# Longer buffer slots, and one operand of the FFN matmuls moved by 32 bytes

## The chip, the cores and the metric

The kernel runs on one core of a Trainium2 chip. The metric is the device time of one execution in microseconds (us), as the median of several runs. A core has a matrix engine (TensorE, PE in the profile, with its weight loads listed apart as PEld), a vector engine (VectorE, DVE), a scalar engine for pointwise functions (ScalarE, ACT), GpSimd (POOL), and a queue that issues most of the DMA transfers (SyncE, SP). All engines work from SBUF, a memory of 128 partitions; where this document gives a place in bytes, it is the place within a partition. Matmuls write to PSUM, eight banks of 512 fp32 columns.

## The reference

One sequence of 512 tokens with 1024 features goes through two layers. Each layer is a token mixer followed by a dense SwiGLU FFN, and each of these four parts has a modulation of its own:

```python
shift, scale, gate = ada_modulation(c, ada_w[i], ada_b[i])
h = rms_norm(x, pre_g[i]) * (1.0 + scale) + shift
y = part(h)                 # attention, FFN, gMLP, FFN
x = x + gate * rms_norm(y, post_g[i])

def swiglu(h, w_gate, w_up, w_down):
    return (jax.nn.silu(h @ w_gate) * (h @ w_up)) @ w_down
```

The mixer of layer 0 is a stick-breaking attention of 16 heads, that of layer 1 a gMLP whose chunks of 128 tokens are mixed by a 128x128 matrix per channel group. The hidden width of the FFN is 2816. Everything is float32.

## The kernel before

**Precision.** Each float32 operand of a large matmul is split into two fp32r parts, a high part h and a low part l (`split`, L112: ScalarE copies, VectorE subtracts). A product is three matmuls, high by high, high by low and low by high (`mm3`, L104). In `mm(o, l, r)` (L92) l is the stationary operand, 128 columns of which are loaded into the array as weights before the matmul, and r the moving operand that streams through. The profile writes a matmul as result<-moving,stationary.

**Memory.** Tiles come from pools laid out one behind the other in each partition. Weights, after their split, lie in `wpool` (tiles wh and wl of 4096 bytes). Behind it the pool `s4` has 28 slots, handed out in turn by `slot` (L53): nearly all that lives longer than a moment is in one, such as h, the attention's operands, the FFN's activations, x, the modulation rows. A slot is 4096 bytes long. All slots and weight tiles start at multiples of 64 bytes.

**h in the FFN.** `boundary` (L419) finishes one part and prepares the next: it norms and modulates 128 tokens, transposes them on TensorE, and splits the result into slots hTh and hTl (L448), each with 4 blocks of 128 features by 256 tokens. `hB` (L413) returns one block, 256 columns or 1024 bytes per partition. Where the next part is an FFN, `boundary` also gets a dictionary S. `sums` (L459) fills it with the operands Sh and Sl (L466): four sums and differences of the quarters of h (two halves of the features by two halves of the tokens).

**The FFN.** The first three of 22 slices of the hidden width are computed directly (`Ffn.unit`, L1002, result gu): 2 x 8 products per 256 tokens. The other 19 go by a scheme with seven products of half size in place of eight (`Ffn.seven`, L1026): gate and up projections of a slice form a 2x2 block matrix, h the other, and the seven products use A11, A12, A22 (blocks of hT) and S1 to S4. Their weights are wh and wl, some of them sums built by `blocks` (L182), and two smaller tiles named b in the profile (b21). Each product is 4 blocks x 3 = 12 matmuls of 256 columns, so a slice is 84 matmuls, in three PSUM banks r1, r2, r3 (together r). In both forms the weights are stationary and h or S is moving:

```python
def product(o, a, b, start, stop):
    for k in range(4):
        h, l = S[a](k)
        wh, wl = W[b](k)
        mm3(o, wh, wl, h, l, start and k == 0, stop and k == 3)
```

Beside this, ScalarE and VectorE split the weights of the next slices, and the SP queue loads them. Where the FFN's down projection (`out_proj`, L491, result y; in the last layer X, Y, Z, W) and the gMLP's v run, it is the other way round: the activations are stationary and the weights are moving, mostly with 512 columns. The gMLP's h (also from `boundary`, with S left out) is moving in u (`u_unit`, L1239) and stationary in v.

The order on TensorE is that of the program; an engine's instructions run in order and wait for semaphores. DMA transfers of weights are issued a few tiles ahead (`wget`, L231), and rows of the modulation matrices (rawada) come in the background (`Bg.run`, L346), partly into slots.

Of the kernel before, what the change touches and what calls it, by code (L numbers as in the profile page):

```python
# [9 lines left out]
F32R = mybir.dt.float32r  # L10
# [3 lines left out]
P = 128  # L14
# [11 lines left out]
PAIRS = (tuple(range(NF)), (2, 4, 0, 6, 7, 1, 9, 10, 3, 5, 8))  # L26
SEVEN = ((2, 4, 6, 7, 9), (2, 4, 6, 7, 9, 10))
NLAST = 3


@with_exitstack
def trunk(ctx: ExitStack, tc: tile.TileContext, A: dict, out: bass.AP):
# [8 lines left out]
    s4 = ctx.enter_context(tc.tile_pool(name="s4", bufs=28))  # L41
# [7 lines left out]
    def nm(s):  # L49
        uid[0] += 1  # L50
        return f"{s}_{uid[0]}"

    def slot(dt, name, a=2, b=512):  # L53
        return s4.tile([P, a, b], dt, tag="s4", name=nm(name))

    def bank(name, tag="b"):
        return psum.tile([P, 512], F32, tag=tag, bufs=6 if tag == "b" else 2, name=nm(name))
# [42 lines left out]
    def transpose(o, i):  # L100
        last_tp[0] = nc.tensor.transpose(o, i, ident)  # L101
        pe_op(last_tp[0])
# [9 lines left out]
    def split(hi, lo, src, hi_dve=False):  # L112
        if hi_dve:
            dve.tensor_copy(hi, src)
        else:
            act.activation(hi, src, AF.Copy)  # L116
        dve.tensor_tensor(lo, src, hi.bitcast(F32), ALU.subtract)
# [177 lines left out]
    for tt in range(NT):  # L295
        xt = slot(F32, "x0", 1, 1024)
        load(xt[:, 0, :], A["x"][tt * P : (tt + 1) * P, :])
        x0.append(xt[:, 0, :])
        if tt == 0:
            identt = consts.tile([P, P], F32, name="identt")  # L300
            load(identt[:], A["consts"][:, 0, :])
            cols = consts.tile([P, 4, KD], F32, name="cols")
            load(cols[:], A["cols"])
        elif tt == 3:
            a0.extend(ada0_raw(0, q) for q in range(2))
# [23 lines left out]
    class Bg:  # L329
# [16 lines left out]
        def run(self):  # L346
            for name, at, s, part in self.parts:
                acc = slot(F32, name, 1, D)[:, 0, :]
                ada[name, at] = acc
                nc.gpsimd.memset(acc, 0.0)  # L350
                load(acc[0:1, :], A["adab"][s, part])
                raws = []
                for k in range(KD + self.lag):
                    if k < KD:
                        if self.slots:
                            raw = slot(F32, "rawada", 1, D)[:, 0, :]
                        else:
                            raw = fwork["raw"].tile([P, D], F32, tag="raw2", name=nm("rawada"))[:]
                        load(raw, A["ada"][s, part, k])
                        raws.append(raw)  # L360
                    if k >= self.lag:
                        ada_stt(acc, raws[k - self.lag], k - self.lag)
                    yield
# [29 lines left out]
    def rms(part, first=None):  # L393

        bias = epsb
        if first is not None:
            bias = small.tile([P, 1], F32, tag="ss", name=nm("ss"))
            dve.tensor_scalar(bias[:], first, 1.0 / D, EPS, ALU.mult, ALU.add)
        sd = small.tile([P, 1], F32, tag="sd", name=nm("sd"))
        last_sqrt[0] = act.activation(sd[:], part, AF.Sqrt, bias=bias[:], scale=1.0 / D)  # L400
        r = small.tile([P, 1], F32, tag="r", name=nm("r"))
        return sd, r

    def new_hT():
        return [
            (slot(F32R, "hTh"), slot(F32R, "hTl")) for _ in range(KD // 2)
        ]
# [11 lines left out]
    def boundary(s, tt, y, xin, hT, S, tag):  # L419

        halves = [slice(0, 512), slice(512, D)]
        sq = [small.tile([P, 1], F32, tag=f"sq{hf}", name=nm("sq")) for hf in range(2)]
        t = npool.tile([P, D], F32, tag="n", name=nm("t"))
        for hf, c in enumerate(halves):
            act.activation(junk[:, c], y[hf][:], AF.Square, accum_out=sq[hf][:])
            if hf == 1:
                sd, r2 = rms(sq[1][:], sq[0][:])
            dve.tensor_tensor(t[:, c], y[hf][:], ada["G", s][:, c], ALU.mult)
        dve.reciprocal(r2[:], sd[:])
        x = xin(tt)  # L430
        dve.scalar_tensor_tensor(x[:], t[:], r2[:, 0:1], x[:], ALU.mult, ALU.add)
        xd[tt] = dram.tile([P, D], F32, tag=f"x{tt}", bufs=2, name=nm("xd"))
        nc.gpsimd.dma_start(out=xd[tt][:], in_=x)
        sx = small.tile([P, 1], F32, tag="sx", name=nm("sx"))
        act.activation(junk[:], x[:], AF.Square, accum_out=sx[:])
        sd, r1 = rms(sx[:])
        dve.tensor_tensor(t[:], x[:], ada["A", s], ALU.mult)
        dve.reciprocal(r1[:], sd[:])
        dve.scalar_tensor_tensor(t[:], t[:], r1[:, 0:1], ada["B", s], ALU.mult, ALU.add)
        late = []  # L440
        for q in range(2):
            ps = bank("tp", tag)
            for k in range(4):
                kk = q * 4 + k
                transpose(ps[:, k * P : (k + 1) * P], t[:, kk * P : (kk + 1) * P])
            a = ps[:].rearrange("p (a b) -> p a b", a=4)
            if tt % 2 == 0:
                hT[tt // 2, q] = (slot(F32R, "hTh", 4, 256), slot(F32R, "hTl", 4, 256))  # L448
            c = slice(tt % 2 * P, (tt % 2 + 1) * P)
            th, tl = hT[tt // 2, q]  # L450
            split(th[:, :, c], tl[:, :, c], a)
            if S is not None and tt < 2:
                if tt == 0:
                    S["c", q] = slot(F32, "c", 4, 256)
                act.activation(S["c", q][:, :, tt * P : (tt + 1) * P], a, AF.Copy)
            late.append(a)
        return lambda: sums(S, tt, late)

    def sums(S, tt, a):  # L459

        if S is None or tt < 2:
            return
        c = slice((tt - 2) * P, (tt - 1) * P)
        if tt == 2:
            for n in "3214":
                S[n] = (slot(F32R, "Sh", 4, 256), slot(F32R, "Sl", 4, 256))  # L466
        f, g = [npool.tile([P, 2, 4, P], F32, tag="n", name=nm("fs")) for _ in range(2)]
        c0, c1 = [S["c", q][:, :, c] for q in range(2)]

        def part(n, f):  # L470
            split(S[n][0][:, :, c], S[n][1][:, :, c], f)

        dve.tensor_tensor(f[:, 0], c0, a[0], ALU.subtract)
        dve.scalar_tensor_tensor(f[:, 1], f[:, 0], -1.0, a[1], ALU.mult, ALU.subtract)
        dve.tensor_tensor(g[:, 0], f[:, 1], c0, ALU.add)
        part("1", g[:, 0])
        part("2", f[:, 1])
        dve.tensor_tensor(g[:, 1], f[:, 1], c1, ALU.add)
        part("4", g[:, 1])
        part("3", f[:, 0])  # L480
# [10 lines left out]
    def out_proj(s, nk, get_act, wkey, J, bg, hT, nxt=(), pre=None, S=None, steps=0, bg2=None):  # L491
# [61 lines left out]
        for n, tt in enumerate((2, 3)):  # L553
            if nxt:
                evacs.append(nxt[n]())
            late.append(boundary(s, tt, y[tt], xin, hT, S, "p" if tt == 3 else "b"))
# [9 lines left out]
    def sqrt_table():  # L566
        with tc.issue_after(last_act[0].ins):
            nc.scalar.preload_act_table_set("sqrt_and_others")
# [42 lines left out]
    hT = new_hT()  # L611
# [129 lines left out]
    with tc.tile_pool(name="att", bufs=1) as att, tc.tile_pool(name="att2", bufs=2) as att2:  # L741
# [60 lines left out]
        for js in (B31, B2, B0):  # L802
            at, n = {}, 0
# [4 lines left out]
            t = att.tile([P, -(-n // 16) * 16], F32, name=nm("ones"))[:, : n - 1]  # L808
# [182 lines left out]
    class Ffn:  # L991
# [97 lines left out]
        def last(self, bg0):  # L1089
# [70 lines left out]
            def common(banks):  # L1160

                us = []
                for s in range(2):
                    u = fpool.tile([P, 4, 256], F32, tag="f13", name=nm("u"))
                    z = [banks["Z", s][:, i * 256 : (i + 1) * 256] for i in range(2)]
                    w = [banks["W", s][:, i * 256 : (i + 1) * 256] for i in range(2)]
                    act.activation(u[:, 0, :], z[0], AF.Copy)
                    dve.tensor_tensor(u[:, 3, :], z[1], u[:, 0, :], ALU.add)
                    dve.tensor_tensor(u[:, 1, :], w[0], u[:, 3, :], ALU.add)
                    dve.tensor_tensor(u[:, 2, :], w[1], u[:, 3, :], ALU.add)  # L1170
                    dve.tensor_tensor(u[:, 3, :], w[0], u[:, 2, :], ALU.add)
                    us.append(u)
                return us
# [18 lines left out]
            for q in range(2):  # L1192
# [4 lines left out]
                for n, p in enumerate(PAIRS[q]):  # L1197
# [4 lines left out]
                    if p in SEVEN[q]:  # L1202
                        seven(now, W, banks, fresh)
                        if p == [i for i in PAIRS[q] if i in SEVEN[q]][-1]:
                            us = common(banks)
                    elif q == 1 and n >= NF - NLAST:
                        tail.append((p, now, W))
                    else:
                        for s in range(2):
                            eight(p, now, W, banks, s, (0, 1), ("X", s) in fresh)  # L1210
                            fresh -= {("X", s), ("Y", s)}
                    if q == 1 and n == NF - NLAST - 2:
                        sqrt_table()
# [278 lines left out]
```

## Time and profile before

| what | us |
|---|---|
| median of 3 runs | 1157.95 (1156.58 to 1157.99) |
| profiled execution | 1156.4 |
| its span, first to last instruction | 1154.6 |
| TensorE busy | 1133.0 |
| VectorE busy | 942.3 |
| ScalarE busy | 588.1 |

The granted clock of TensorE is 0.996 in the mean. The profile's groups of instructions give a line, an engine, an operation, result<-operands and the count, then busy time and the mean length of one in ns. A matmul is a pipeline: the profile's length of one is longer than the distance to the next, so the distance between starts is what counts. The chain of work that ended last lists pieces with their start, their length, and what they are; a piece of matmuls divided by its count gives the distance. Rows of a tile give the shortest, median and longest instruction in ns.

### The profile page before, as it was taken

How to read it: one execution, taken by the hardware profiler on the slowest of the kernel's cores; microseconds unless marked ns; L12 is line 12 of the kernel's file. 1: busy time of each engine (PE TensorE's matmuls, PEld its weight loads, DVE VectorE, ACT ScalarE, POOL GpSimd, SP SyncE). 2: the span in 40 equal slices, each digit the busy share in tenths (PEclk: the TensorE clock that was granted, in tenths of full speed). 3: DMA queues.
4: the chain of work that ended last, by engine and by line, in shares of the span. 5: the costliest groups of instructions: out<-in, count | busy, mean ns of one | idle time of the engine just before them, and what ended most of it. 6: DMA issues, size and time to landing. Idle time of an engine off the chain costs nothing.

```text
span 1154.6 us, 18784 instructions
## 1 busy us (share of the span) xinstructions
PE 1133.0 (98%) x7532; PEld 1022.3 (89%) x7532; DVE 942.3 (82%) x1214; ACT 588.1 (51%) x977; POOL 23.9 (2%) x43
## 2 busy tenths in 40 slices
PE   6999999999999999999999999999999999999997
PEld 4778888788999999998877898988999999999996
DVE  4988999866998889879686955668979898789996
ACT  6444454645655555554142633526555555565752
POOL 0010000000000000000000100001000000000000
PEclk9999999999999999999999999999999999999999
DMA  8855433114425343338887465324333433223242
GB/s 313 330 183 170 140 111 128 73 56 146 146 92 165 129 148 127 119 118 279 276 283 239 149 231 168 111 70 155 106 125 129 164 129 125 77 91 94 90 163 94
DMA packets 50812, 174.43 MB, mean 151 GB/s; under 512 B 5786, under 2 KB 9114, under 8 KB 50724
## 3 DMA queue, kind: packets, MB, share of 16 engines
q1 hardware_dynamic: 48996, 166.94, 42.7%
q0 software_dynamic: 1728, 6.29, 1.4%
q8 instruction: 59, 0.97, 0.3%
q14 instruction: 29, 0.24, 0.1%
HBM read 164.82 MB, written 8.39 MB: 150 GB/s over the span
## 4 chain that ended last, share of the span: by engine, by line
PE 84%; DMA 6%; DVE 6%; ACT 2%; issue 1%; SPq 0%; DVEq 0%; ACTq 0%
PE r L93 33%; PE y L93 9%; PE v L93 8%; PE pqk L93 7%; PE gu L93 5%; DMA rawada<-in_ada 4%; PE X L93 4%; PE Y L93 3%; PE u L93 3%; PE av L93 3%; PE z L93 2%; PE W L93 1%; PE Z L93 1%; PE tw L101 1%; PE tp L101 1%
## 5 line engine op out<-in xcount | busy, mean ns | idle before, releaser
L93 PE MATMUL r<-Sh,wh 128*128 128x256 f32 x608 | 172.1, 283 | 0.0
L93 PE MATMUL r<-Sl,wh 128*128 128x256 f32 x608 | 172.1, 283 | 0.0
L93 PE MATMUL r<-Sh,wl 128*128 128x256 f32 x608 | 172.1, 283 | 0.0
L93 PE MATMUL y<-wh,as 128*128 128x512 f32 x480 | 150.8, 391 | 0.8 <-DVE G L69 0.8
L159 ACT ACTIVATE wh<-raw 128x1024 fp32r<-128x1024 f32 x87 | 91.6, 1058 | 116.3 <-PE y L93 58.6
L69 DVE TENSOR_TENSOR wl<-f,wh 128x1024 fp32r<-128x1024 f32 x87 | 106.2, 1220 | 39.8 <-ACT wh L116 39.8
L116 ACT ACTIVATE wh<-f 128x1024 fp32r<-128x1024 f32 x87 | 92.2, 1060 | 89.9 <-PE r L93 65.6
L160 DVE TENSOR_TENSOR wl<-raw,wh 128x1024 fp32r<-128x1024 f32 x87 | 105.8, 1219 | 38.5 <-ACT wh L159 34.5
L93 PEld LDWEIGHTS r<-Sh,wh 128*128 128x128 f32 x608 | 116.7, 192 | 0.0
L93 PEld LDWEIGHTS r<-Sl,wh 128*128 128x128 f32 x608 | 116.7, 192 | 0.0
L93 PEld LDWEIGHTS r<-Sh,wl 128*128 128x128 f32 x608 | 116.7, 192 | 0.0
L93 PEld LDWEIGHTS y<-wh,as 128*128 128x128 f32 x480 | 90.1, 188 | 19.7 <-DVE G L69 1.3
L93 PE MATMUL y<-wl,as 128*128 128x512 f32 x240 | 93.7, 390 | 0.0
L93 PE MATMUL r<-hTh,wh 128*128 128x256 f32 x304 | 87.8, 292 | 0.0
L93 PE MATMUL r<-hTl,wh 128*128 128x256 f32 x304 | 85.4, 282 | 0.0
L93 PE MATMUL r<-hTh,wl 128*128 128x256 f32 x304 | 81.0, 283 | 0.0
L93 PE MATMUL r<-hTh,b 128*128 128x256 f32 x304 | 61.0, 283 | 0.0
L93 PEld LDWEIGHTS r<-hTh,wh 128*128 128x128 f32 x304 | 57.9, 191 | 2.4 <-DVE gu L69 0.7
L93 PEld LDWEIGHTS r<-hTl,wh 128*128 128x128 f32 x304 | 58.1, 191 | 0.1
L116 ACT ACTIVATE wh<-rawx 128x1024 fp32r<-128x1024 f32 x38 | 40.3, 1060 | 33.9 <-PE r L93 31.8
L93 PEld LDWEIGHTS r<-hTh,wl 128*128 128x128 f32 x304 | 55.9, 191 | 0.0
L93 PE MATMUL gu<-hTh,wh 128*128 128x256 f32 x192 | 54.6, 285 | 0.0
(266 smaller groups left out, 3026.7 us busy)
## 6 DMA issues: line engine op xcount, KB each, us to landing
rawada<-in_ada SPq DMA_DIRECT2D x80, 512.0 KB, 4.6
rawy<-in_wy SPq DMA_DIRECT2D x38, 512.0 KB, 3.5
rawx<-in_wx SPq DMA_DIRECT2D x38, 512.0 KB, 4.3
raw<-in_wdown SPq DMA_DIRECT2D x22, 512.0 KB, 4.5
raw<-in_wdn SPq DMA_DIRECT2D x22, 512.0 KB, 3.5
raw<-in_wqk SPq DMA_DIRECT2D x16, 512.0 KB, 4.4
ada<-in_ada0p SPq DMA_DIRECT2D x12, 512.0 KB, 8.1
raw<-in_wgu SPq DMA_DIRECT2D x12, 512.0 KB, 3.5
```

The lines of the kernel that those rows point to most:

```text
L69: b = getattr(nc.vector, op)(*args, **kw)
L93: b = nc.tensor.matmul(o, l, r, start=start, stop=stop, skip_group_check=True)
L101: last_tp[0] = nc.tensor.transpose(o, i, ident)
L116: act.activation(hi, src, AF.Copy)
L159: act.activation(h[:], raw[:], AF.Copy)
L160: nc.vector.tensor_tensor(l[:], raw[:], h[:].bitcast(F32), ALU.subtract)
```

## The change

Slots of `s4` become 1040 fp32 elements (4160 bytes) long, that is 64 bytes longer. `slot` returns a view of the first 1024 elements, or of 1024 elements from `at` on. For the two FFNs, the slots of h (hTh, hTl) and of its sums (Sh, Sl from `sums`) are asked for with `at = 8` elements, 32 bytes. The h of the gMLP, and the operands named Sh and Sl that the last FFN's down projection builds for itself, stay at the start of their slots.

```diff
+ODD = 8
...
-    def slot(dt, name, a=2, b=512):
-        return s4.tile([P, a, b], dt, tag="s4", name=nm(name))
+    def slot(dt, name, a=2, b=512, at=0):
+
+        t = s4.tile([P, 1040], dt, tag="s4", name=nm(name))
+        return t[:, at : at + a * b].rearrange("p (a b) -> p a b", a=a)
...
             if tt % 2 == 0:
-                hT[tt // 2, q] = (slot(F32R, "hTh", 4, 256), slot(F32R, "hTl", 4, 256))
+                at = 0 if S is None else ODD
+                hT[tt // 2, q] = (slot(F32R, "hTh", 4, 256, at), slot(F32R, "hTl", 4, 256, at))
...
         if tt == 2:
             for n in "3214":
-                S[n] = (slot(F32R, "Sh", 4, 256), slot(F32R, "Sl", 4, 256))
+                S[n] = (slot(F32R, "Sh", 4, 256, ODD), slot(F32R, "Sl", 4, 256, ODD))
```

The 28 slots together take 28 x 64 = 1792 bytes more per partition; the pools behind them start that much later.

## The prediction

> **What bounds the kernel now.** I read the page first, then the groups of matmuls by shape, the chain of work that ended last, four stretches of time, and last the single starts of matmuls.
>
> ```profile
> span 1154.6 us, 18784 instructions
> PE 1133.0 (98%) x7532; PEld 1022.3 (89%) x7532; DVE 942.3 (82%) x1214; ACT 588.1 (51%) x977; POOL 23.9 (2%) x43
> ...
> PE r L93 33%; PE y L93 9%; PE v L93 8%; PE pqk L93 7%; PE gu L93 5%; DMA rawada<-in_ada 4%; PE X L93 4%; PE Y L93 3%; PE u L93 3%; PE av L93 3%; PE z L93 2%; PE W L93 1%; PE Z L93 1%; PE tw L101 1%; PE tp L101 1%
> ```
>
> TensorE has work in 98% of the span, and a third of the chain that ends last is the products called r, which are the middle of the two FFNs. The change touches the moving operand (named first after the arrow) of exactly these groups:
>
> ```profile
> L93 PE MATMUL r<-Sh,wh 128*128 128x256 f32 x608 | 172.1, 283 | 0.0
> L93 PE MATMUL r<-Sl,wh 128*128 128x256 f32 x608 | 172.1, 283 | 0.0
> L93 PE MATMUL r<-Sh,wl 128*128 128x256 f32 x608 | 172.1, 283 | 0.0
> ...
> L93 PE MATMUL r<-hTh,wh 128*128 128x256 f32 x304 | 87.8, 292 | 0.0
> L93 PE MATMUL r<-hTl,wh 128*128 128x256 f32 x304 | 85.4, 282 | 0.0
> L93 PE MATMUL r<-hTh,wl 128*128 128x256 f32 x304 | 81.0, 283 | 0.0
> L93 PE MATMUL r<-hTh,b 128*128 128x256 f32 x304 | 61.0, 283 | 0.0
> L93 PE MATMUL gu<-hTh,wh 128*128 128x256 f32 x192 | 54.6, 285 | 0.0
> L93 PE MATMUL gu<-hTh,wl 128*128 128x256 f32 x192 | 54.3, 283 | 0.0
> L93 PE MATMUL gu<-hTl,wh 128*128 128x256 f32 x192 | 54.3, 283 | 0.0
> ...
> L93 PE MATMUL r<-hTl,b 128*128 128x256 f32 x152 | 43.0, 283 | 0.0
> ```
>
> That is 3 x 608 + 4 x 304 + 152 = 3192 matmuls r and 3 x 192 = 576 matmuls gu. The 283 ns is a matmul with its pipeline. What it costs is the distance from one start to the next, which the chain gives as length over count:
>
> ```profile
> 306.58 22.31 PE gu L93 x186
> 328.89 181.34 PE r L93 x1500
> ...
> 743.85 6.65 PE sv L93 x60
> ...
> 762.84 25.04 PE y L93 x110
> ...
> 815.20 22.32 PE gu L93 x186
> 837.52 181.37 PE r L93 x1500
> ```
>
> A 256-column matmul costs 22.31 / 186 = 119.9 ns (gu) and 181.34 / 1500 = 120.9 ns (r). One of 512 columns costs 25.04 / 110 = 227.6 ns (y). So 256 columns more cost 107.7 ns, or 0.42 ns each, and 119.9 - 107.7 = about 12 ns per matmul do not depend on its length. The change can reach these 12 ns. One of 128 columns costs 6.65 / 60 = 110.8 ns (sv), far over 54 + 12: there another thing sets the pace, the load of 128 columns of weights that each matmul has, so 110.8 ns is the floor for the 256-column matmul too.
>
> ```profile
> 329.00:511.00 182.00, 182.00 (x1506) 181.18 (x1505) 153.02 (x206) 97.42 (x162) 0.00 (x0) 1.00 0.39 127
> 837.00:1019.00 182.00, 182.00 (x1507) 181.22 (x1506) 150.79 (x201) 96.97 (x162) 0.00 (x0) 1.00 0.37 122
> 815.00:837.00 22.00, 22.00 (x186) 22.00 (x185) 21.40 (x33) 11.28 (x18) 0.00 (x0) 1.00 0.22 74
> 292.00:329.00 37.00, 36.96 (x309) 36.72 (x308) 35.51 (x49) 22.55 (x39) 1.68 (x3) 1.00 0.43 146
> ```
>
> The columns are TensorE, weight loads, VectorE, ScalarE, GpSimd, granted clock, DMA. In the two r stretches (first two rows) TensorE is busy all the time at full clock, VectorE for 153.02 / 182 = 84%. Whatever a start costs there goes straight into the span. In the gu stretch at 815 us VectorE is busy 21.40 of 22 us, so a gain there is partly hidden behind it; a loss is not.
>
> The starts at the beginning of a block of r, where TensorE had waited:
>
> ```profile
> 338.71 0.39 PE L93 MATMUL r<-hTh,wh 128*128 128x256 f32 x1
> 338.94 0.28 PE L93 MATMUL r<-hTl,wh 128*128 128x256 f32 x1
> 339.05 0.29 PE L93 MATMUL r<-hTh,wl 128*128 128x256 f32 x1
> 339.18 0.28 PE L93 MATMUL r<-hTh,wh 128*128 128x256 f32 x1
> 339.29 0.28 PE L93 MATMUL r<-hTl,wh 128*128 128x256 f32 x1
> 339.41 0.28 PE L93 MATMUL r<-hTh,wl 128*128 128x256 f32 x1
> 339.53 0.28 PE L93 MATMUL r<-hTh,wh 128*128 128x256 f32 x1
> ```
>
> After the wait the distances are uneven (0.11 to 0.13 us), and then they lock at 0.12 us and stay there. Same instructions, same operands, different distance: some of the 12 ns depends on how the reads of the moving operand and of the next weights fall against each other.
>
> **The change part by part.** No instruction is added, removed or reordered; the work of each is the same.
>
> (1) h and S of the two FFNs start 32 bytes into their slots. Before, every moving operand of r and gu starts at a multiple of 1024 bytes from its slot, and every weight block at a multiple of 512; slots and weights start at multiples of 64. So in 3768 matmuls both streams begin on the same place within 64 bytes, and after the change they begin half of it apart. No row of before has a 256-column fp32r matmul with such an offset. The nearest rows are these:
>
> ```profile
> L93 PEld LDWEIGHTS r<-hTh,wh x304: 186/192/193, 328.6 to 1032.2; 128*128 128x128 f32 x152
> ...
> L101 PEld LDWEIGHTS tw<-identt,ga x160: 137/140/146, 105.4 to 255.1; 128*128 128x128 f32 x160
> ...
> L69 DVE TENSOR_TENSOR ga<-left x24: 694/1222/1229, 76.9 to 245.8; 128x1027 f32<-128x1027 f32 x8, 128x513 f32<-128x513 f32 x8, 128x1025 f32<-128x1025 f32 x8
> ...
> L101 PEld LDWEIGHTS tp<-identt,t x96: 137/140/143, 280.5 to 814.8; 128*128 128x128 f32 x96
> ...
> 280.80 0.82 PE L101 MATMUL tp<-identt,t 128*128 128x128 f32 x6
> 281.38 0.71 PE L93 MATMUL y<-wh,o 128*128 128x512 f32 x2
> ```
>
> The weights from ga start 0, 4, 8 or 12 bytes past a multiple of 64 (the blocks of ga are spaced by one element more than a multiple of 128); those from t start on it. Both loads take 140 ns. The identity, moving operand of these transposes, stands 32 bytes past a multiple of 64 (behind the 32 bytes of cT), and the last transpose, started at 280.80 + 0.82 - 0.27 = 281.35, is followed by the next matmul 0.03 us later. So an odd start by itself shows no price, which speaks against a loss. But in r the weight loads vary from 186 to 193 ns while their operands are alike; read with the uneven starts above, that is interplay between the two reads.
>
> Bounds per matmul: the gain ends at the floor, 120 - 110.8 = 9.2 ns. For a loss, 1024 bytes at +32 touch 17 pieces of 64 bytes in place of 16; if the extra piece costs its sixteenth of 107 ns, that is 6.7 ns. I take the value nearest to what the same instructions already show, the short steps of 0.11 us: 113 ns, a gain of 7 ns. For r 3192 x 7 = 22.3 us. For gu 576 x 7 = 4.0 us, of which I count half because of VectorE: 2.0 us. VectorE would then be busy for 84% x 120 / 113 = 89% of r, still not the bound. If it did become the bound, its waits for ScalarE's weight splits would be what is late next.
>
> The Trainium skill ("TensorE: Matmul & The Clock Gate", section "Back-to-back issue gap") gives N / 2.4 + 2.5 ns for a warm matmul alone, which is 109.2 ns for 256 columns. The trace shows 120 ns; by the page's figure the two parts of (1) would save up to 3768 x 10.8 = 41 us, an estimate that ignores the floor seen in sv.
>
> (2) Slots of 4160 bytes. 28 slots x 64 = 1792 bytes: the slots move against each other by multiples of 64, the pools behind them by 1792. VectorE and ScalarE read and write slots everywhere. ga<-left, both of whose sides are shifted by 4 bytes, takes 1222 ns for some 1026 elements, so a shifted operand costs them nothing. DMA rows into slots stay 4096 bytes long. If the landing of rawada grew by 5%, the 4% of the chain that it holds (46 us) would grow by 2.3 us. Nothing in the page speaks for such a growth; I take zero and keep 2 us for the range.
>
> (3) Writes of h and S at the offset: a few dozen splits on ScalarE and VectorE, zero by the same row.
>
> Sum: 22.3 + 2.0 = 24.3 us less than the profiled execution's own 1156.4 us (span 1154.6), that is 1132.1. This execution is 1.5 us under the median of the runs shown (1157.95); I forecast 1133 us. The bounds: at the floor 3192 x 9.2 + half of 576 x 9.2 = 32 us, so 1124 us; with the extra piece 3768 x 6.7 = 25 us more, so 1181.6 us.
>
> **The rivals.** *Nothing happens.* The fixed 12 ns would belong to the array, to the exchange of one set of weights for the next, and not to reads. For it: once locked, the distance is 120 ns for every pair of operands, whether b, wh or wl, and 12 ns at 512 columns as at 256. Against it: the uneven starts. Time 1156 us, within 2 us. By the Trainium skill ("SBUF — State Buffer", section "Who interferes with whom") TensorE reads its moving operand and its weights through two independent ports; by that rule this rival is right. The constant 120 ns agrees with it, the uneven starts do not.
>
> *Slower.* The run of 1024 bytes that no longer starts on a 64-byte place touches one piece more, and the array waits for it at every start. Place: all r and gu, 3768 x 6.7 ns = 25 us, 1181.6 us. It decides as soon as the extra piece costs over 0.6 ns (2.3 us / 3768) without a gain to offset it. For it: TensorE has no slack in the r stretches. Against it: the identity's row, where the odd start is followed after 0.03 us. A milder form is the lock falling on the longer of the uneven steps, 0.125 us: 3768 x 5 = 19 us, 1175 us.
>
> *A part of the gain.* The lock moves to 118 ns, the mean of the five steps from 338.94 to 339.53: 2 x 3192 = 6 us, 1150 us.
>
> **How the numbers follow.** The forecast near 113 ns has 0.30, a part of it 0.10, the floor 0.04: faster 0.44. Nothing 0.26. The extra piece 0.17, a milder loss or a slower DMA by (2) 0.13: slower 0.30. The runs of before lie between 1156.58 and 1157.99, so 0.2% (2.3 us) is about what a measurement can tell. The range is 1126 to 1182, from near the floor to the extra piece; outside I leave 0.05 on each side. Since it holds cases of both signs: the forecast's own range is 1126 to 1140.
>
> **What would show it.** In the changed profile the r pieces of the chain should have about 171 us for 1500 matmuls in place of 181, starts of r every 0.11 us, and weight loads of r nearer 188 than 192 ns; u, sv, y and v keep their distances, and the pair of r stretches shows VectorE at 88 to 90%. If r still has 0.12 us per start, the first rival is right; at 0.125 to 0.127 the second. If r is unchanged and the time moves, look at (2): the landings of rawada and x, and the distances of y and av, whose weights lie in slots. The prediction fails if the short steps after a wait come from a buffer that is filled once and not from the way two reads meet.

## The result

The changed kernel takes 1154.68 us (median of 14 runs, 1153.09 to 1159.38). The kernel before, run beside it, takes 1156.73 us (14 runs, 1154.22 to 1159.83). The ratio is 0.9988, with a 95% interval of 0.9975 to 1.0001: no difference that can be told. The forecast was 1133 us.

The profiled execution after has a span of 1154.0 us (before 1154.6). From its page: the engines, the shares of the chain that ended last, and the groups of r, of y, and of r's weight loads:

```profile
span 1154.0 us, 18784 instructions
PE 1130.8 (98%) x7532; PEld 1015.1 (88%) x7532; DVE 942.6 (82%) x1214; ACT 587.9 (51%) x977; POOL 23.9 (2%) x43
...
PE r L96 33%; PE y L96 16%; PE v L96 8%; PE pqk L96 7%; PE X L96 4%; PE gu L96 4%; PE Y L96 3%; PE u L96 3%; PE av L96 3%; PE z L96 2%; PE Z L96 1%; PE W L96 1%; PE tw L104 1%; PE ab L96 1%; PE tp L104 1%; PE sv L96 1%
...
L96 PE MATMUL r<-Sh,wh 128*128 128x256 f32 x608 | 170.8, 281 | 0.0
...
L96 PE MATMUL y<-wh,as 128*128 128x512 f32 x480 | 153.0, 395 | 0.2 <-DVE G L72 0.2
...
L96 PEld LDWEIGHTS r<-hTh,wh 128*128 128x128 f32 x304 | 57.1, 188 | 3.8 <-DVE gu L72 0.8
```

The same row of y on the page of before:

```profile
L93 PE MATMUL y<-wh,as 128*128 128x512 f32 x480 | 150.8, 391 | 0.8 <-DVE G L69 0.8
```

The matmuls of r are 2 ns shorter (283 to 281), and the weight loads in the row shown last 3 ns (191 to 188), which the prediction had named as a sign. But y, whose operands were not placed anywhere else in their slots, is 4 ns longer (391 to 395). (The chain's share of y, 16% here and 9% on the page before, says nothing: the kernel before, run again, has 14%.) The chain of work that ended last says the same (start, length, what, count). After:

```profile
306.81 22.05 PE gu L96 x186
328.86 179.86 PE r L96 x1500
...
663.41 16.89 PE u L96 x143
...
744.09 6.65 PE sv L96 x60
...
763.13 25.59 PE y L96 x110
...
1129.66 4.16 PE X L96 x18
```

Before, for the two pieces that the prediction doesn't show:

```profile
663.40 17.15 PE u L93 x143
...
1130.77 4.11 PE X L93 x18
```

Divided by the counts: r 120.9 to 119.9 ns, gu 119.9 to 118.5, u 119.9 to 118.1, sv 110.8 as it was, y 227.6 to 232.6, X 228.3 to 231.1. So matmuls with 256 columns became 1 to 2 ns cheaper, and those with 512 columns 3 to 5 ns dearer. The first stretch of r (TensorE, weight loads, VectorE, ScalarE, GpSimd, clock, DMA) shows TensorE busy all the time, as before:

```profile
329.00:511.00 182.00, 182.00 (x1517) 180.47 (x1517) 154.65 (x209) 97.96 (x163) 0.00 (x0) 1.00 0.38 128
```

**The balance by stage.** For each stage I add up the distances from each matmul's start to the next one's. Distances up to 132 ns (245 ns for 512 columns) give the mean spacing; what the stage takes beyond count times spacing is waiting. In us, with the mean spacing in ns in brackets:

| stage | before | after | difference |
|---|---|---|---|
| r, 3192 matmuls | 386.2 [119.9] | 383.2 [118.4] | -3.0 |
| gu | 70.1 [119.9] | 69.8 [118.7] | -0.3 |
| u | 46.4 [119.9] | 46.6 [118.2] | +0.2 |
| X, Y, Z, W with 256 columns | 55.4 [119.9] | 54.4 [117.8] | -1.0 |
| y | 212.8 [227.7] | 215.0 [231.9] | +2.2 |
| X, Y with 512 columns | 60.0 [227.6] | 60.8 [230.6] | +0.8 |
| pqk | 94.5 [229.5] | 95.2 [231.6] | +0.7 |
| v | 91.7 [228.1] | 91.3 [232.0] | -0.4 |

The sum is -0.8 us, and the spans differ by 0.6 us. In r, 3192 x 1.53 ns = 4.9 us of streaming is gained, and 1.9 us of it is lost again to more waiting (3.4 to 5.3 us). The change did not fail to act: it acted on nearly every stage, in both directions.

### The profile page after: what moved, and what is told of

The parts are those of the page before. It is cut to its first block, busy times and chain, and to the rows that moved or that the text cites. A ratio compares the mean times of both kernels' runs of the same rounds, so it can differ in the third digit from the quotient of the medians.

```text
span 1154.0 us, 18784 instructions
## 1 busy us (share of the span) xinstructions
PE 1130.8 (98%) x7532; PEld 1015.1 (88%) x7532; DVE 942.6 (82%) x1214; ACT 587.9 (51%) x977; POOL 23.9 (2%) x43
## 4 chain that ended last, share of the span: by engine, by line
PE 90%; DVE 4%; DMA 2%; ACT 2%; issue 1%; SPq 0%; DVEq 0%; ACTq 0%
PE r L96 33%; PE y L96 16%; PE v L96 8%; PE pqk L96 7%; PE X L96 4%; PE gu L96 4%; PE Y L96 3%; PE u L96 3%; PE av L96 3%; PE z L96 2%; PE Z L96 1%; PE W L96 1%; PE tw L104 1%; PE ab L96 1%; PE tp L104 1%; PE sv L96 1%
## 5 line engine op out<-in xcount | busy, mean ns | idle before, releaser
L96 PEld LDWEIGHTS r<-Sh,wl 128*128 128x128 f32 x608 | 114.3, 188 | 0.0
```

The costliest lines, as they stand in the source:

```text
L96: b = nc.tensor.matmul(o, l, r, start=start, stop=stop, skip_group_check=True)
```

## The experiments

### Does the spacing belong to the addresses or to the execution?

Both kernels were run once more, unchanged (e1_before_again, e2_after_again).

> The kernel before, once more, with a profile of its own. Theory A (placement): the steady distance of 0.120 us between 256-column matmuls belongs to the addresses, so it is back here: 1500 matmuls of r in 181.3 us, y of 512 columns at 227.6 ns, weight loads of r at 192 ns. Theory B (execution): the profile of after has uneven distances (mean 118.3 ns at 256 columns, 231 ns at 512) in every stage, also in those whose addresses are as before, so the pattern belongs to the execution or the chip; then this run may show 1500 of r in about 180 us and y at 231 ns with unchanged addresses.

> The changed kernel once more. Theory A: 1500 matmuls of r in 179.9 us again, y at 231 to 233 ns, ratio 0.9975 to 1.0001. Theory B: the distances are those of the run of before beside it on this chip, whichever they are, and the ratio is 1 within 0.2%.

Measured: one run of the kernel before took 1153.53 us. The changed one took 1157.36 us (12 runs); its ratio to the 29 runs of the kernel before beside it (1155.04 us) is 1.0008 (0.9991 to 1.0024). The first two rows are from the chain of the kernel before, run again, and the last two from that of the changed kernel, run again:

```profile
325.60 181.33 PE r L93 x1500
...
758.92 25.04 PE y L93 x110
```

```profile
839.64 178.52 PE r L96 x1487
...
761.55 25.59 PE y L96 x110
```

That is 120.9 and 227.6 ns, then 120.1 and 232.6 ns, as in the first profiles. The spacing comes back with the kernel, and the two kernels differ in nothing but addresses, so it belongs to them.

### The slots alone, and the 32 bytes alone

e3_slots_only is the changed kernel without the 32 bytes:

```diff
-ODD = 8
+ODD = 0
```

> The slots of 4160 bytes alone; h and S stay at the start of their slots. If the offset of 32 bytes is what shortened r, r is back at 120.9 ns (181.3 us for 1500) and the time is 1 to 2 us longer than that of the changed kernel. If the skew of the slots did it, r is at 119.9 ns and the time equals that of the changed kernel. Under theory B it shows the pattern of its neighbours and ratio 1 within 0.2%.

Measured: 1154.42 us, ratio 1.0002 (0.9985 to 1.0019).

```profile
762.00 25.59 PE y L96 x110
...
836.77 180.18 PE r L96 x1500
```

r 120.1 ns, y 232.6 ns, mean spacing of r 118.2 ns (118.4 with the 32 bytes): the pattern of the changed kernel is all there without the 32 bytes. The longer slots make it, which the prediction had costed at nothing.

e4_weights_32 keeps the slots' length and puts the weights 32 bytes apart from them instead, with a pad ahead of the pool `wpool` and another behind it. From the first FFN on, every sixth weight tile comes from `wpool2`, which lies behind both pads, as the slots and b do; these weights keep the distance of before:

```diff
+    pad0 = ctx.enter_context(tc.tile_pool(name="pad0", bufs=1))
+    pad0.tile([P, 8], F32, name="pad0")
...
+    pad1 = ctx.enter_context(tc.tile_pool(name="pad1", bufs=1))
+    pad1.tile([P, 8], F32, name="pad1")
```

> Slots as before, but the pool of split weights starts 32 bytes later, so that weights against h and S stand 32 bytes apart in r, gu, u, and in y, v, X, Y with moving and stationary exchanged. If two streams that begin on the same place of 64 bytes disturb each other, all these stages get faster at once: up to 7 ns for some 4500 matmuls, 30 us. If an odd start of the moving operand costs, y, v, X and Y get slower by up to 7 ns each, some 14 us. Under theory B ratio 1 within 0.2%.

Measured: 1155.39 us, ratio 1.0009 (0.9991 to 1.0027); mean spacing of r 117.6 ns, of y 232.6 ns. Within r, the matmuls on b (distance as before) keep 119.5 ns, and the others take 117.4 in the mean: the spacing changes from product to product with the place of the weights. An offset of 32 bytes alone gains 2 to 3 ns per matmul in r, not 7, and costs y as much as the slots do.

### What a distance between the operands costs, by itself

e5_distances runs cells of 96 matmuls with nothing else beside them. In each cell the moving operand starts a given number of bytes further than the weights:

```python
for k in range(REP):
    h, l = mov("mh", mh, k), mov("ml", ml, k)
    a, b = wt("wh", wh, k), wt("wl", wl, k)
    mm(o[:, :n], a, h, k == 0, False)
    mm(o[:, :n], a, l, False, False)
    mm(o[:, :n], b, h, False, k == REP - 1)
```

> A kernel of matmuls alone, in cells of 96 (high by high, low by high, high by low, as in the FFN); it leaves out the whole computation and copies x to the output. Cells q have 256 columns, cells s 512; in a to m the moving operands start 0, 4, 16, 32, 48, 64, 96, 128, 192, 256, 288, 384, 448 bytes past the place of the weights within 512 bytes; n has the weights 32 bytes past, o a mixture (moving high 192, moving low 0, weights high 64, weights low 448); qz and sz repeat the first cells. If the distance between matmuls follows from the two start addresses alone: qa and qz 120 ns, sa and sz 226.7 ns, every other q shorter (115 to 118.5 ns) and every other s longer (230 to 234 ns), as in the run with the weights moved. If other engines' accesses make the pattern: all q alike and all s alike.

From its chain, cells of 256 columns (qa, qb, qd, qi, qj: distance 0, 4, 32, 192, 256 bytes) and of 512 columns (sa, sb, sd, sf, si, sj: 0, 4, 32, 64, 192, 256 bytes):

```profile
27.80 11.52 PE qa L74 x96
39.32 11.84 PE qb L74 x96
...
62.36 11.20 PE qd L74 x96
...
119.13 10.91 PE qi L74 x96
130.04 11.50 PE qj L74 x96
...
197.99 21.78 PE sa L74 x96
219.77 22.78 PE sb L74 x96
...
264.80 22.40 PE sd L74 x96
...
309.59 21.97 PE sf L74 x96
...
376.37 22.39 PE si L74 x96
398.75 21.80 PE sj L74 x96
```

Mean spacing in the steady part of each cell:

| distance, bytes | 256 columns, ns | 512 columns, ns |
|---|---|---|
| 0, 256 | 120.0 | 226.7 |
| 4 | 123.3 | 237.3 |
| 32 | 116.7 | 233.3 |
| 64 | 117.8 | 228.9 |
| 96 | 120.0 | 233.3 |
| 128 | 118.6 | 233.3 |
| 192, 448 | 113.3 | 233.3 |
| 288 | 117.8 | 233.3 |
| 384 | 118.6 | 232.4 |

0 agrees with 256 and 192 with 448; 32 and 288, and 128 and 384, agree within 1.1 ns. So the spacing repeats after 256 bytes, not after 64, though not always to the nanosecond. Distance 0 is the best place for 512 columns and one of the worse ones for 256; 192 is the best for 256 and close to the worst for 512. Moving the weights does the same as moving the other operand: weights 32 bytes further give 118.3 ns with 256 columns, and the moving operand 224 further, in e8_pairs below, gives the same. The kernel before had all slots and weights at distance 0. Slots of 4160 bytes start at 0, 64, 128 and 192 of 256 in turn, so every operand in a slot gets one of four distances.

e8_pairs repeats such cells with the places of high and low parts that the changed kernel has:

> Matmuls alone again (the whole computation is left out), now with the very places of high and low parts that the changed kernel gives to r: cells qa to qi as with slots of 4160 bytes alone, qj to qr the same 32 bytes further, qs to qu with both at 224, 176, 208; sb to sg the 512-column cells with the stationary operand displaced (64 and 128, 192 and 128, 64 and 0, 128 and 192, 32, 192). If the places alone explain the changed kernel, the mean of qa to qi is about 118, that of qj to qr 118.4 ns, so the 32 bytes add nothing to what the longer slots do; sb to se 231 to 233 ns, sg 228.9 ns.

Measured: nine pairs of slots without the 32 bytes give 117.8 to 121.1 ns, mean 118.6; nine with them 117.0 to 120.0 ns, mean 118.4; the pairs of 512 columns 226.7 ns at distance 0, 228.9 at 64, and 231.1 to 233.3 ns in the others. The kernel shows 118.2 (e3), 118.4 (after) and about 232 ns. The places alone account for its spacings within 0.5 ns. One cell here repeats a place of e5 and differs: all moving operands at 128 give 120.0 ns, where e5 had 118.6. So the distance doesn't fix the spacing wholly.

### The best distance for r, in the kernel

e6_weights_64 has slots as before and both weight pools 64 bytes further, so that h - weights is 192 in the sense of the cells; e7_weights_192 moves them by 192 bytes:

```diff
+SHIFT = 64
...
+    shift("pad0", SHIFT)
...
+    shift("pad1", 256 - SHIFT)
...
+    shift("pad2", SHIFT)
```

> Slots as before (4096 bytes); all split weights (both pools and b) start 64 bytes further, so that S and h stand 192 past the weights within 256 where they move, and weights 64 past the slots where they move. If the two start addresses alone set the distance, the cells give: r, gu, u (4152 matmuls) 113.3 in place of 120 ns, 27.7 us less; Z, W, X, Y of 256 columns (462) 117.8, 1.0 us less; y, X, Y, v of 512 columns (1367) 228.9 in place of 226.7, 3.0 us more; pqk, pq, pk (384) 233.3, 2.6 us more. Sum 23 us less, ratio about 0.980; 22 us if the gain in gu is half hidden. If other engines or other waits take the place of the matmuls, ratio over 0.99.

> The same with the weights 192 bytes further, the mirror image. By the cells: r, gu, u 117.8 ns, 9.1 us less; Z, W, X, Y of 256 columns 113.3, 3.1 us less; y, X, Y, v of 512 columns 233.3, 9.1 us more; pqk, pq, pk 228.9, 0.9 us more. Sum 2.2 us less, ratio 0.998: almost as large a shift as the run with 64, and almost nothing in time. If any displacement helped, it would equal that run.

Measured: e6 1149.56 us, ratio 0.9944 (0.9922 to 0.9965); e7 1152.81 us, ratio 0.9978 (0.9961 to 0.9995), a time as expected, though r runs at 116.9 ns in place of 117.8. e6 is faster than both kernels, but by 6 us where 22 to 23 were expected. Its spacing in r is 115.3 ns in the mean, so streaming gains 3192 x 4.66 = 14.9 us. Yet r is only 6.0 us shorter (380.2), since its waiting went from 3.4 to 12.3 us. Two things show.

First, the spacing falls on one of two values, slice by slice: 22 of the 38 slices run at about 113.4 ns and the others at about 117.8, on the same distance. The same two values mix in r of e7, at distance 64, where 7 slices run at 113.3 ns and 31 at 117.8. The two pieces of gu in the chain of e6 have the same instructions and the same distance:

```profile
309.15 21.09 PE gu L99 x186
...
813.66 21.91 PE gu L99 x186
```

21.09 / 186 = 113.4 and 21.91 / 186 = 117.8 ns.

Second, TensorE now waits for VectorE. In the chain of e6, VectorE's sums of weight blocks (f) stand between the pieces of r:

```profile
377.00 1.49 DVE f L75 x2
...
456.49 1.83 DVE f L75 x3
```

and the list of waits (engine, what, for whom: us in total, times, longest) has this row (on the page after, quoted above, the weight loads of r wait 0.8 us for gu):

```profile
PEld r L99 <- DVE gu L75: 8.3, 23, 1.0
```

VectorE is busy for 156.16 of the 182 us from 329 to 511, 86%, while TensorE's share falls from 182.00 to 179.79 us:

```profile
329.00:511.00 182.00, 179.79 (x1521) 176.56 (x1520) 156.16 (x211) 98.33 (x164) 0.00 (x0) 1.00 0.40 131
```

VectorE isn't full, and is still late.

### Is it VectorE that eats the gain?

e9_before_light and e10_w64_light leave out two of VectorE's additions per slice, on the kernel before and on e6; their output is not the reference's. What the expectations of these runs and of e12 call the waits (9.6 and 21.0 us) is, counted as in the tables here, 3.4 and 12.3 us.

```diff
-        f24 = fp.tile([P, KD, P], F32, tag="f24", bufs=1, name=nm("f24"))
-        dve.tensor_tensor(f24[:, 0:4, :], f13[:, 0:4, :], xr[:, 4:8, :], ALU.add)
-        dve.tensor_tensor(f24[:, 4:8, :], f24[:, 0:4, :], yr[:, 0:4, :], ALU.add)
...
-        split(t24[0][:], t24[1][:], f24[:])
+        split(t24[0][:], t24[1][:], f13[:])
```

> The kernel before, with the weights of the second and fourth Strassen product of each slice split without the two additions that make them (left out: those additions, about 1.37 us of VectorE work in each slice of gu, so the output isn't the reference's). It is the base for the same omission on the kernel with the weights 64 bytes further. Theory (part of what a faster TensorE gains is eaten by longer waits on VectorE): with VectorE lighter and TensorE's spacing unchanged at 120 ns, only the waits that are there now can go, 9.6 us in r, so 1146 to 1156 us, ratio 0.992 to 1.000. Rival (VectorE does not count): no change, 1.000.

> The same omission on the kernel with slots as before and the weight pools 64 bytes further. Theory: VectorE no longer holds TensorE up, so the waits in r fall from 21.0 us to about those of the base, and if all slices then take the 113.4 ns spacing the time is 15 to 22 us below the base (1125 to 1140 us). Rival: the spacing still falls on 113.4 or 117.8 ns slice by slice, mean about 115 ns: 3192 x 4.6 ns = 15 us of streaming less in r, and the time 11 to 16 us below the base. Second rival: the waits don't depend on VectorE's load, and the time is only 6 us below the base, as it is without the omission.

e11_w64_again is e6 once more.

> The kernel with slots as before and the weight pools 64 bytes further, once more. If its gain belongs to the addresses: 0.994 again, about 1149 us. If each slice of r falls on 113.4 or 117.8 ns by how it restarts after its wait, the slices mix again, but not the same ones need to be fast. If the first was a chance of the chip, 1.000.

Measured beside each other: e9 1155.75 us, ratio 0.9995 (0.9977 to 1.0012); e10 1143.42 us, ratio 0.9874 (0.9850 to 0.9898); e11 1147.09 us, ratio 0.9913 (0.9894 to 0.9932). With the spacing of before, a lighter VectorE is worth nothing. With the faster spacing it is worth 3.7 us more (e10 against e11). From e9 to e10 the time falls by 12.3 us; without the omission the same move of the weights gave 6 us in e6 and 9.5 us here. The chain of e10 has no VectorE between its pieces of r:

```profile
384.74 39.31 PE r L99 x336
...
463.40 9.80 PE r L99 x84
...
502.17 10.13 PE r L99 x84
```

Here a slice takes 9.8 us, or 10.1 us in one that runs at 117.8 ns (7 of 38 do), where the kernel before takes 181.34 / 1500 x 84 = 10.2 us. The full theory (15 to 22 us) asked for 113.4 ns everywhere; the mean is 114.3, so the first rival's 11 to 16 us is what came. Against e11 beside it, e10's r has 4.6 us less waiting (9.3 for 13.8) and 1.2 us less streaming, as 31 slices were fast and not 28. The profile is of e10's shortest run (1139.92 us). Its waiting in r is still 5.8 us more than e9's (3.5), so the load taken off is a part of the waiting and not all of it. Some 0.3 us is left at the end of most slices. The list of waits puts it down to VectorE's gu, which takes the sums over from PSUM (5.7 us in e10, 0.6 in e9):

```profile
PEld r L99 <- DVE gu L75: 5.7, 22, 0.9
```

Why this handover shows at the shorter spacing and hardly at the longer one was not tried.

In e11, 28 of 38 slices were fast, not 22. X, Y, Z and W with 256 columns, whose weights move and stand at distance 64, ran at 113.7 ns, where e6 with the same places had 117.8. The gain comes back, and its size with how the slices fall.

e12_w64_pool gives VectorE less to do in another way: GpSimd makes the low part of b21 in e6.

```diff
-        split(b21[0][:], b21[1][:], yr[:, 0:4, :])
+        act.activation(b21[0][:], yr[:, 0:4, :], AF.Copy)
+        nc.gpsimd.tensor_tensor(
+            out=b21[1][:], in0=yr[:, 0:4, :], in1=b21[0][:].bitcast(F32), op=ALU.subtract
+        )
```

> The kernel with the weight pools 64 bytes further, and the subtraction for the low part of b21 moved from VectorE to GpSimd: VectorE has 0.68 us less in each slice and computes the same. Theory (VectorE's lateness holds TensorE up): the waits in r shrink from 21.0 us by 3 to 10 us, and the time is 1140 to 1147 us, ratio 0.987 to 0.992. Rival: GpSimd takes longer over the same subtraction (above 1.5 us) and shares its way to memory with VectorE, so the b21 weights come late instead, and the time is 1150 to 1165 us.

Measured: 1159.81 us, ratio 1.0021 (1.0006 to 1.0036): the rival's case. By the groups of e12 and then of e6:

```profile
L195 POOL TENSOR_TENSOR b<-rawy,b 128x512 fp32r<-128x512 f32 x38 | 63.8, 1681 | 545.4 <-ACT b L194 545.4
...
L75 DVE TENSOR_TENSOR f<-f,rawx 128x512 f32<-128x512 f32 x38 | 43.5, 1145 | 0.0
```

```profile
L75 DVE TENSOR_TENSOR f<-f,rawx 128x512 f32<-128x512 f32 x38 | 26.0, 685 | 0.0
...
L75 DVE TENSOR_TENSOR b<-rawy,b 128x512 fp32r<-128x512 f32 x38 | 26.0, 684 | 5.2 <-ACT b L122 5.2
```

GpSimd takes 1681 ns for what took VectorE 684, and VectorE's own sum beside it grows from 685 to 1145 ns, 38 x 460 ns = 17.5 us of the 26.0 us that were to be saved. That mean is of two kinds: 23 of the 38 sums run beside GpSimd's subtraction and take 1450 ns, the 15 others 677 ns. The Trainium skill ("SBUF — State Buffer", section "Who interferes with whom") says that an instruction of VectorE with two inputs in SBUF contends with one of GpSimd that reads SBUF; these rows agree. TensorE waits longer for VectorE than in e6 (8.3 us there), and for its gu, not for b as the rival had it:

```profile
PEld r L99 <- DVE gu L75: 22.5, 35, 1.3
```

### The change's own idea with other sizes

e13_h_192 lengthens the slots by 256 bytes and places h and S 192 bytes into them; e14_slots_4352 lengthens the slots alone. Both have 26 slots.

```diff
-ODD = 8
+ODD = 48
...
-    s4 = ctx.enter_context(tc.tile_pool(name="s4", bufs=28))
+    s4 = ctx.enter_context(tc.tile_pool(name="s4", bufs=26))
...
-        t = s4.tile([P, 1040], dt, tag="s4", name=nm(name))
+        t = s4.tile([P, 1088], dt, tag="s4", name=nm(name))
```

> The change with other sizes: slots 256 bytes longer in place of 64, h and S 192 bytes into them in place of 32, and 26 slots in place of 28 so that all still fits. If the spacing follows the distance between the two operands modulo 256 bytes, r and gu fall on 113.4 or 117.8 ns slice by slice, as with the weights 64 bytes further (the same distance), r is 5 to 8 us shorter with its waits, y keeps 227.7 ns and the 256-column X, Y, Z and W keep 120 ns: 6 to 10 us less than the run with 26 slots alone. If only the weights' place counts, r keeps 120 ns, ratio to that run 1.000. If two slots fewer cost time, both runs show it.

> Slots 256 bytes longer, nothing moved inside them, 26 slots in place of 28. By the period of 256 bytes every spacing is that of before (r 119.9 ns, y 227.7 ns, X to W 119.9 ns), ratio 1.000 but for what two slots fewer cost (waits, at most some us). If any lengthening of the slots changes the spacing, r shows 118 and y 232 ns, as with 64 bytes more.

Measured: e13 1148.13 us, ratio 0.9941 (0.9923 to 0.9959); e14 1156.93 us, ratio 1.0026 (1.0010 to 1.0041). Two slots fewer cost a little; on that base the 192 bytes are worth 8.8 us. The chain of e14, and then that of e13:

```profile
304.72 22.32 PE gu L96 x186
...
762.95 25.04 PE y L96 x110
...
837.78 181.34 PE r L96 x1500
```

```profile
304.83 21.91 PE gu L96 x186
...
486.29 9.81 PE r L96 x84
...
759.47 25.04 PE y L96 x110
...
811.91 21.11 PE gu L96 x186
```

With slots a whole 256 bytes longer every spacing is that of before: 22.32 / 186 = 120.0, 25.04 / 110 = 227.6, 181.34 / 1500 = 120.9 ns. With h and S at 192 bytes, r is 8.3 us shorter than e14's (377.9 against 386.2; spacing 114.7), and y keeps 227.6 ns. Here it is the first gu that runs at 117.8 ns and the second at 113.5, the other way round than in e6.

| kernel | spacing r, ns | r in all, us | waiting in it, us | spacing y, ns |
|---|---|---|---|---|
| before | 119.9 | 386.2 | 3.4 | 227.7 |
| after | 118.4 | 383.2 | 5.3 | 231.9 |
| e6 weights +64 | 115.3 | 380.2 | 12.3 | 230.4 |
| e11 the same, again | 114.7 | 379.8 | 13.8 | 230.4 |
| e10 the same as e6, VectorE lighter | 114.3 | 374.1 | 9.3 | 230.4 |
| e12 the same as e6, GpSimd helps | 114.7 | 391.6 | 25.5 | 230.4 |
| e13 h +192 | 114.7 | 377.9 | 11.9 | 227.6 |
| e14 slots +256 | 119.9 | 386.2 | 3.4 | 227.7 |

## Why the prediction was wrong

**The mechanism of step (1) held.** Part of the 12 ns that don't depend on a matmul's length hangs on where moving operand and weights lie against each other. That it is their reads that meet is the nearest explanation; no run looks inside. The cells show 113.3 ns for 256 columns, the value that the step took from the short steps after a wait, and e6 and e13 reach 113.4 ns in the kernel. A spacing that holds over 96 matmuls isn't the ending that the prediction feared, a buffer that is filled once. But those short steps were seen at distance 0, and no run ties them to the 113.3 ns at distance 192, so that the two agree may be luck.

**The size of step (1) failed, and this is the term that missed.** Of the 24.3 us forecast it held 22.3 for r and 2.0 for gu; r became 3.0 us shorter and gu 0.3. The step took 7 ns because both streams then begin half of 64 bytes apart. The period is 256 bytes and 32 is not the good place: a distance of 32 gives 116.7 ns in a cell, 3.3 ns less than distance 0. In the changed kernel h and S are not at one distance either, since the slots walk through four places. r measured 118.4 ns, a gain of 1.5 ns, and 118.2 ns without the 32 bytes: what r gained came with the longer slots of step (2), and the 32 bytes added nothing to it.

**Step (2) failed too, by less.** Slots that move against each other by multiples of 64 were costed at zero, and u, y and v were to keep their distances. u went from 119.9 to 118.2 ns, y from 227.7 to 231.9, v from 228.1 to 232.0. The price is on the 512-column matmuls, whose best distance is 0: y +2.2, X and Y +0.8, pqk +0.7 and v -0.4 us, 3.3 us in all (v and y also waited less, by some 2 us each). It cancels most of the 4.1 us that the 256-column stages gained, so no difference is left that can be told. The part of step (2) on DMA held: rawada lands in 4.5 us on the page after, 4.6 before. The row that step (2) leaned on was VectorE's; nothing in it speaks for TensorE. The sentence that names y as a place to look was right, the price of zero was not.

**"An odd start by itself shows no price" was too wide.** The rows behind it were transposes with 128 columns, which start 109 to 110 ns apart, at the floor that the prediction read from sv (110.8 ns, before and after). A distance of 4 bytes costs 3.3 ns with 256 columns and 10.6 ns with 512.

**"VectorE still not the bound" failed as an argument by share.** VectorE was at 85% in r (154.65 / 182), not 88 to 90%, as the gain was small. But in e6 TensorE waits for it at 86%. A share under 90% didn't say that its results come in time; e10 bears that out.

**The rivals.** "Nothing happens" had the time (1156 us, within 2) by luck and for the wrong reason: the spacing does depend on places, and gains and prices happen to cancel. One of its supports was no evidence: the 12 ns come from the line through 256 and 512 columns, so they are the same at both by construction. The Trainium skill ("SBUF — State Buffer", section "Who interferes with whom") says that TensorE waits for no one at its ports and gives the weights a read port of their own; the cells, with no other engine at work, go from 113.3 to 123.3 ns with the distance alone. So no other engine is needed for the effect, and TensorE's two operands are not independent in time here; where they meet is not shown. "Part of the gain" had the spacing (118 ns) and missed what the other stages give back. The extra piece of 64 bytes was not seen: with 32 bytes the spacing is shorter, not longer, at 256 columns; at 512 columns 32 bytes cost 6.6 ns, but 192 bytes, whole pieces, cost the same.

## What to carry to other kernels

Where TensorE is busy throughout, the distance between moving operand and weights modulo 256 bytes is worth measuring in cells of bare matmuls before any padding is chosen, for each matmul length, since the best place for one length can be a bad one for another. The cells give a bound and not the gain: e6 brought 6 us where they promised 22 to 23. Padding of a shared ring of buffers moves every operand in it: a whole period leaves the others alone, and an offset inside the slot then moves only what should move. A gain on the busiest engine counts only as far as the next engine's results arrive, and that is read from the waits at the points of handover, not from its share of busy time.

## What the runs showed of the hardware

The fp32r matmuls here repeat their spacing after 256 bytes of distance, to about 1 ns, between 113.3 and 123.3 ns with 256 columns and between 226.7 and 237.3 ns with 512. Why 192 is best for the one and 0 for the other isn't settled; the cells give the prices only.

At distance 192, and at 64 too (e7), the spacing of 256 columns in the kernel holds either about 113.4 or about 117.8 ns, in most cases for a whole slice of 84 matmuls or a whole stage, with the same instructions and distance (gu in e6, 21.09 and 21.91 us for 186). A new value is taken up between slices, mostly after a wait. What decides between them was not found: the same kernel had 16 slow slices of 38 in one execution and 10 in the next (e6, e11). In the cells, which follow one another without a wait, 192 gave 113.3 ns and 64 gave 117.8.
